# One pass over all tokens, layouts prepared on the host, and sums of squares on VectorE, in a two-layer decoder step on eight cores

## The chip, the cores and the metric

The kernel runs on all eight cores of one Trainium2 chip. Each core works on one prompt of 2048 tokens and on 128 sample tokens, and nothing is exchanged between cores. The metric is the device time of the slowest core in microseconds (us). Engines are named as in the profile: PE is TensorE (matmul), PEld its weight loads, DVE VectorE, ACT ScalarE, POOL GpSimd, SP SyncE.

Executions of a program on eight cores fall into two states. In the slow one the cores of one die, or of both, show a lower granted clock and the time is some per cent longer. Only fast runs are compared here.

## The reference

Activations are `x` with 1024 features. Weights are shared by prompt and sample tokens.

```python
def _swiglu(h, w_gate, w_up, w_down):            # 1024 -> 2816 -> 1024
    return (jax.nn.silu(h @ w_gate) * (h @ w_up)) @ w_down

for layer in range(2):
    x = x + 0.5 * _swiglu(_rmsnorm(x, norm_g[layer, 0]), ...)
    h = _rmsnorm(x, norm_g[layer, 1])
    # even layer: gelu(h @ w_u) * spatial_gate(layernorm(gelu(h @ w_v)))
    #             beside a gated 3-tap causal convolution; then @ e_w_out
    # odd layer:  p = h @ o_w_in; causal means of the last 2, 4, 8, 16 rows
    #             minus p; per group @ pool_w, * pool_scale; then @ o_w_out
    x = x + mixer(h)
    x = x + 0.5 * _swiglu(_rmsnorm(x, norm_g[layer, 2]), ...)
y = _rmsnorm(x, final_norm_g)
```

There are four feed-forward stages (FFN), one even and one odd mixer, and seven norms.

## The kernel before

The tokens are cut in two halves of 1024 and 1152, and the whole network runs first on one, then on the other, so every weight is read twice. Activations live transposed (features on partitions). Three parts matter for the argument.

`x` arrives row by row and is transposed by TensorE, 136 times; `y` goes back the same way.

```python
def tr(e, i=i, half=half, bk=bk):
    for k in range(4):
        c = half * 4 + k
        ins = e.transpose(banks[bk][:, k * 128:(k + 1) * 128],
                          big[:, i * 1024 + c * 128:i * 1024 + (c + 1) * 128], ident[:])
    return ins
```

A norm needs, for each token, the sum of squares over 1024 features. ScalarE squares each of the eight chunks of 128 features, and TensorE adds them up, across chunks and across partitions, by multiplying with a matrix of 1/1024. Six of the seven norms do this; the last one's squares are summed by ScalarE, after the transposes of `y`:

```python
P.add("act", ... e.activation(out=buf, in_=xT[:, dc, a:a + n], func=AF.Square), ...)
P.add("pe",  ... e.matmul(bank[:, 0:n], onesm[:], buf, start=(dc == 0), stop=(dc == NCH - 1)), ...)
```

The down projection of an FFN runs all 22 chunks of hidden features into one bank (PSUM, where matmuls accumulate), and VectorE adds the result to `x` once:

```python
for f in range(f0, f1):
    ins = e.matmul(po[:, 0:n], sd[:, f, :], aT[:, f, a:a + n], start=(f == 0), stop=(f == NF - 1))
...
P.add("dve", ... e.scalar_tensor_tensor(out=xT[:, dc, a:a + n], in0=po[:, 0:n], scalar=0.5, in1=xT[:, dc, a:a + n], ...))
```

## Time and profile before

| | before |
|---|---|
| time, median of the first 5 runs | 2565.91 us (2562.0 to 3019.57) |
| profiled span, slowest core | 2561.0 us |
| TensorE busy, matmuls | 2430.3 us, 13009 |
| TensorE idle | 131 us |
| VectorE busy | 792.0 us |
| read from memory | 337.63 MB |

The run of 3020 us is slow. The lines behind the table stand in the prediction below. To read them: a busy TensorE is not a TensorE at its peak, so the time is split in three parts. First come columns times their spacing (the stream), then busy time above that spacing (mostly matmuls at about double the spacing, called half clock here), then idle time.

### The profile page before, as it was taken

To read this page: it belongs to the slowest core of one execution; us is meant where nothing else is said; L and a number is where in the kernel's file an instruction comes from. 1 tells how busy PE (TensorE), PEld (TensorE's weight loads), DVE (VectorE), ACT (ScalarE), POOL (GpSimd) and SP (SyncE) were. 2 spreads that over 40 slices of the span, in tenths; PEclk is the share of its full clock that TensorE was granted. 3 is DMA by queue.
4 is the path that set the end of the run, shared out by engine and by line. 5 is a ranking of instruction groups with operands and counts; after the bars stand their busy time and mean duration, and the time that the engine had idled before them with its cause. 6 is when DMAs were issued, how large, how long until landed. Compare 5 with 4: busy or idle time off the path is not lost.

```text
span 2561.0 us, 35190 instructions; the slowest of 8 cores (2545.0 to 2561.0 us)
## 1 busy us (share of the span) xinstructions
PE 2430.3 (95%) x13009; PEld 1287.6 (50%) x13009; DVE 792.0 (31%) x1329; ACT 597.3 (23%) x1134; POOL 305.7 (12%) x319
## 2 busy tenths in 40 slices
PE   6999899999999889997899989999999999899997
PEld 3444344444444334444466645566655665456664
DVE  3211553112221552113322147522132212742213
ACT  3111322112111242102311132411121111531102
POOL 2101111111101111111010102111111111001110
PEclk8999999999999999998899999999999999999998
DMA  8667366567566555668255544555675555436472
GB/s 149 83 67 73 42 91 82 68 65 91 67 72 68 74 66 67 72 72 174 58 72 58 59 58 63 90 67 62 58 87 67 61 55 67 59 50 82 57 75 77
DMA packets 418126, 187.20 MB, mean 73 GB/s; under 512 B 186251, under 2 KB 412119, under 8 KB 417944
## 3 DMA queue, kind: packets, MB, share of 16 engines
q0 software_dynamic: 410048, 162.55, 54.3%
q1 hardware_dynamic: 6616, 17.69, 2.1%
q10 hardware_dynamic: 1296, 4.72, 0.6%
q8 instruction: 108, 1.77, 0.3%
q14 instruction: 58, 0.48, 0.1%
HBM read 337.63 MB, written 10.29 MB: 136 GB/s over the span
## 4 chain that ended last, share of the span: by engine, by line
PE 87%; DVE 5%; ACT 2%; issue 2%; DMA 2%; SPq 1%; POOL 1%; ACTq 0%; DVEq 0%; POOLq 0%
PE ps L529 25%; PE ps L532 25%; PE ps L573 24%; PE ps L637 4%; DVE hT L504 2%; PE ps L482 2%; PE ps L928 1%; DVE big L949 1%; PE ps L808 1%; PE ps L704 1%; PE ps L750 1%; PE ps L810 1%; DMA big<-xs 1%; PE ps L831 1%; SPq L392 1%
## 5 line engine op out<-in xcount | busy, mean ns | idle before, releaser
L529 PE MATMUL ps<-hT,wslot 128*128 128x384 bf16 (+1 forms) x3520 | 723.6, 349 | 15.7 <-DVE big L538 15.0
L532 PE MATMUL ps<-hT,wslot 128*128 128x384 bf16 (+1 forms) x3520 | 721.9, 348 | 0.0
L573 PE MATMUL ps<-big,wslot 128*128 128x384 bf16 (+1 forms) x3520 | 659.5, 348 | 0.0
L538 DVE TENSOR_TENSOR big<-ps,stmp 128x384 bf16<-128x384 f32 (+1 forms) x440 | 268.2, 611 | 1015.9 <-ACT stmp L536 1008.5
L529 PEld LDWEIGHTS ps<-hT,wslot 128*128 128x128 bf16 x3520 | 344.6, 98 | 322.7 <-issue 23.7
L532 PEld LDWEIGHTS ps<-hT,wslot 128*128 128x128 bf16 x3520 | 345.5, 98 | 305.9 <-issue 5.5
L573 PEld LDWEIGHTS ps<-big,wslot 128*128 128x128 bf16 x3520 | 345.7, 98 | 304.2 <-issue 3.4
L536 ACT ACTIVATE stmp<-ps 128x384 f32<-128x384 f32 (+1 forms) x440 | 234.6, 533 | 1024.8 <-PE ps L532 1023.1
L578 DVE SCALAR_TENSOR_TENSOR xT<-ps,xT 128x384 f32<-128x384 f32 (+1 forms) x160 | 97.6, 610 | 495.3 <-PE ps L573 479.9
L473 ACT ACTIVATE sqbuf<-xT 128x384 bf16<-128x384 f32 (+1 forms) x240 | 131.8, 563 | 499.9 <-DVE xT L578 416.8
L299 POOL DMA_DIRECT2D wslot<-wg x88 | 77.2, 878 | 1162.0 <-PE ps L532 804.6
L299 POOL DMA_DIRECT2D wslot<-wd x64 | 85.9, 1342 | 711.3 <-PE ps L532 413.0
L504 DVE SCALAR_TENSOR_TENSOR hT<-xT,cT,rs 128x384 bf16<-128x384 f32 (+1 forms) x240 | 145.5, 668 | 65.1 <-ACT rs L495 64.0
L482 PE MATMUL ps<-sqbuf,onesm 128*128 128x384 bf16 (+1 forms) x240 | 76.5, 373 | 15.9 <-ACT sqbuf L473 15.2
L299 POOL DMA_DIRECT2D wslot<-wu x88 | 78.0, 887 | 0.0
L928 PE MATMUL ps<-hT,wslot 128*128 128x384 bf16 (+1 forms) x320 | 62.6, 359 | 5.3 <-DVE big L892 5.3
L637 PE MATMUL ps<-mixT,wslot 128*128 128x384 bf16 (+1 forms) x320 | 65.0, 347 | 2.4 <-DVE xT L641 2.4
L641 DVE TENSOR_TENSOR xT<-ps,xT 128x384 f32<-128x384 f32 (+1 forms) x80 | 48.5, 608 | 60.5 <-PE ps L637 60.5
L637 PE MATMUL ps<-hT,wslot 128*128 128x384 bf16 (+1 forms) x320 | 65.6, 350 | 0.2 <-ACT hT L1005 0.2
L949 DVE TENSOR_TENSOR big<-big 128x1038 f32<-128x1038 f32 (+3 forms) x40 | 49.4, 1236 | 10.2 <-ACT big L933 7.7
L1045 ACT ACTIVATE rt<-ps 128x512 f32<-128x512 f32 x17 | 10.0, 587 | 171.1 <-PE ps L1040 161.0
L928 PEld LDWEIGHTS ps<-hT,wslot 128*128 128x128 bf16 x320 | 32.1, 101 | 35.3 <-issue 10.0
(134 smaller groups left out, 968.6 us busy)
## 6 DMA issues: line engine op xcount, KB each, us to landing
wslot<-wg POOLq DMA_DIRECT2D x88, 512.0 KB, 6.2
wslot<-wu POOLq DMA_DIRECT2D x88, 512.0 KB, 8.1
wslot<-wd POOLq DMA_DIRECT2D x64, 704.0 KB, 7.9
wslot<-ewin POOLq DMA_DIRECT2D x16, 512.0 KB, 7.4
big<-xp SPq DMA_DIRECT2D x8, 512.0 KB, 10.1
wslot<-ewout POOLq DMA_DIRECT2D x8, 512.0 KB, 8.8
wslot<-owin POOLq DMA_DIRECT2D x8, 512.0 KB, 7.1
wslot<-owout POOLq DMA_DIRECT2D x8, 512.0 KB, 6.8
```

The lines of the kernel that those rows point to most:

```text
L299: res.append(e.dma_start(out=dst, in_=src))
L473: P.add("act", lambda e, dc=dc, a=a, n=n, buf=buf: e.activation(out=buf, in_=xT[:, dc, a:a + n], func=AF.Square), r=K("x", dc, a, n), w=[( ...
L482: P.add("pe", lambda e, dc=dc, n=n, buf=buf, bank=bank: e.matmul(bank[:, 0:n], onesm[:], buf, start=(dc == 0), stop=(dc == NCH - 1)), r=[( ...
L504: P.add("dve", lambda e: e.scalar_tensor_tensor(out=dst, in0=xT[:, c, a:a + n], scalar=cT[:, nidx * 8 + c:nidx * 8 + c + 1], in1=rs[:, 0:n ...
L529: e.matmul(pg[:, 0:n], sg[:, c, fi * 128:(fi + 1) * 128], hT[:, c, a:a + n], start=(c == 0), stop=(c == NCH - 1))
L532: ins = e.matmul(pu[:, 0:n], su[:, c, fi * 128:(fi + 1) * 128], hT[:, c, a:a + n], start=(c == 0), stop=(c == NCH - 1))
L536: P.add("act", lambda e, k=k, n=n, pg=pg: e.activation(out=stmp[k][:, 0:n], in_=pg[:, 0:n], func=AF.Silu), r=[("ps", k)], w=[("stmp", k)])
L538: P.add("dve", lambda e, k=k, f=f, a=a, n=n, pu=pu: e.tensor_tensor(out=aT[:, f, a:a + n], in0=pu[:, 0:n], in1=stmp[k][:, 0:n], op=ALU.mul ...
L573: ins = e.matmul(po[:, 0:n], sd[:, f, :], aT[:, f, a:a + n], start=(f == 0), stop=(f == NF - 1))
L578: P.add("dve", lambda e, dc=dc, a=a, n=n, po=po: e.scalar_tensor_tensor(out=xT[:, dc, a:a + n], in0=po[:, 0:n], scalar=0.5, in1=xT[:, dc, ...
L637: ins = e.matmul(po[:, 0:n], sw[:, c, (di % 2) * 128:(di % 2 + 1) * 128], src[:, c, a:a + n], start=(c == 0), stop=(c == NCH - 1))
L928: ins = e.matmul(pb[:, 0:n], sw[:, c, (di % 2) * 128:(di % 2 + 1) * 128], hT[:, c, a:a + n], start=(c == 0), stop=(c == NCH - 1))
```

## The change

Its intent is to shorten TensorE's stream and to keep it fed. The new kernel makes one pass over all 2176 tokens in five blocks, so weights are read once. The host delivers `x` already transposed and takes `y` transposed, and it packs the weights in the order in which they are used. The sums of squares move to VectorE, and only the last step, across partitions, stays on TensorE, in the type float32r (fp32r below). The tile for hidden features holds 8 of the 22 chunks for 2176 tokens, so FFN and down projection run in three parts, each with its own addition to `x`. The product of the pool weights and the output weights of the odd mixer is formed first. The causal sums become a scan. The diff, cut to its core:

```diff
-SBS = [dict(idx=0, Tp=1024, Ts=0, T=1024, poff=0, blocks=[(0, 512), (512, 512)]),
-       dict(idx=1, Tp=1024, Ts=128, T=1152, poff=1024, blocks=[(0, 384), (384, 384), (768, 384)])]
+BL = [(0, 384), (384, 512), (896, 384), (1280, 512), (1792, 384)]
+PARTS = [(0, 6), (6, 8), (14, 8)]            # hidden chunks per part
...
-    # x: DMA by rows, 136 transposes on PE, copies out by ACT and DVE
+    P.add("sp", ... e.dma_start(out=xT(o0, o1), in_=x_in[:, o0:o1]) ...)      # host has transposed it
...
-    P.add("pe", ... e.matmul(bank[:, 0:n], onesm[:], buf, start=(dc == 0), stop=(dc == NCH - 1)) ...)  # 8 per block
+    P.add("dve", ... e.tensor_tensor(out=acc(0, n), in0=acc(0, n), in1=dst, op=ALU.add) ...)           # 7 per block
+    P.add("pe", ... e.matmul(banks[bk][:, 0:n], ones_t[:], accr_t[k][:, 0:n], start=True, stop=True) ...)  # 1 per block, fp32r
...
-    # odd mixer: doubling additions for the causal sums, pool weights on all tokens, scale, output weights
+    P.add("dve", ... e.tensor_tensor_scan(out=S_(0, pn), data0=pext(16 + a, ...), data1=pext(16 + a - w_, ...),
+                                          op0=ALU.add, op1=ALU.subtract) ...)
+    # V = (pool_w * pool_scale) @ o_w_out, 32 matmuls of 512 columns, then one projection with V
```

Normalizations (`x * g * rs`, one VectorE instruction per chunk) wait in a queue `hq`. The last down part takes one out per group, but only while block 0 has some. The rest follows when the next stage asks for them.

```python
last_rate[0] = 2 if final else (1 if any(x[0] == 0 for x in hq) else 0)
down(j0 if dc < 4 else j1, b, dc, nf, True)      # ends with tick(last_rate[0]): so many out of hq
```

## The prediction

> **What bounds the kernel now.** First the page, then the granted clocks, then the windows, then the chain that ended last, then the waits of TensorE.
>
> ```profile
> span 2561.0 us, 35190 instructions; the slowest of 8 cores (2545.0 to 2561.0 us)
> ...
> PE 2430.3 (95%) x13009; PEld 1287.6 (50%) x13009; DVE 792.0 (31%) x1329; ACT 597.3 (23%) x1134; POOL 305.7 (12%) x319
> ...
> HBM read 337.63 MB, written 10.29 MB: 136 GB/s over the span
> ...
> PE 87%; DVE 5%; ACT 2%; issue 2%; DMA 2%; SPq 1%; POOL 1%; ACTq 0%; DVEq 0%; POOLq 0%
> ```
>
> TensorE is busy for 95% of the span and no other engine passes 31%; the chain that ended last is TensorE work for 87%. The kernel is bound by its matmul stream, so a change can win in only two ways: fewer matmul columns, or less time in which TensorE is idle or at a low clock. The chain in order of time gives the rate of the stream:
>
> ```profile
> 60.37 1.73 PE ps L529 x8
> ...
> 214.48 9.50 PE ps L573 x44
> ...
> 1410.05 1.30 PE ps L532 x8
> ...
> 1438.49 10.72 PE ps L573 x66
> ```
>
> Columns: start, length, what. A 512-column matmul takes 1.73 / 8 = 216 ns, a 384-column one 10.72 / 66 = 162.4 ns. The larger means in the list of groups (348 ns) are latencies of overlapping instructions and are not used. With the block widths 512, 512 | 384, 384, 384 of before the mean is (2 x 216.2 + 3 x 162.4) / 5 = 183.9 ns. The windows show where the time is that is not this stream:
>
> ```profile
> core 1: us, PE busy (x) PEld busy (x) DVE busy (x) ACT busy (x) POOL busy (x), PEclk, DMA share, GB/s
> 0.00:60.00 60.00, 39.98 (x169) 21.94 (x170) 21.27 (x33) 21.82 (x37) 13.43 (x26) 0.89 0.93 159
> 60.00:195.00 135.00, 135.00 (x627) 61.23 (x626) 26.98 (x39) 23.29 (x39) 16.28 (x17) 1.00 0.59 71
> ...
> 260.00:370.00 110.00, 98.11 (x457) 43.98 (x455) 66.54 (x114) 37.02 (x57) 22.30 (x22) 0.95 0.48 64
> ...
> 875.00:960.00 85.00, 76.88 (x327) 31.84 (x326) 53.23 (x70) 35.19 (x62) 8.74 (x10) 0.92 0.48 62
> ...
> 1190.00:1242.00 52.00, 30.97 (x148) 18.96 (x146) 23.45 (x42) 25.12 (x63) 1.75 (x2) 0.71 0.67 189
> ```
>
> Inside a feed-forward stage (60 to 195) TensorE is busy for 135 of 135 us at clock 1.00: nothing to win there except columns. The idle time, 2561 - 2430 = 131 us, lies at the start, in the mixers (260 to 370, 875 to 960 and their second copies), at the seam between the two halves of the tokens (1190 to 1242: 21 us idle, clock 0.71) and at the end. Few of the waits are for data from memory:
>
> ```profile
> PE ps L482 <- ACT sqbuf L473: 15.2, 9, 3.1
> PE ps L529 <- DVE big L538: 15.0, 8, 2.5
> PE ps L432 <- DMA big<-xp: 12.1, 6, 3.3
> ```
>
> The first is the norm statistics, the second the product that frees a bank, the third the load of x, not of weights.
>
> **What the Trainium skill says.** (1) "TensorE: Matmul & The Clock Gate", section "Wait — 56ns, not 53.3ns?": warm matmuls follow each other after N / 2.4 GHz + about 2.5 ns, 215.7 ns for 512 columns. The trace agrees (216). So after, as before, width alone sets the stream. (2) Same page, "HAM oscillation — how this bites in real kernels": after gaps of more than about 3.4 us the array restarts at half clock. The trace agrees in kind: clock 0.71 to 0.95 just in the windows with gaps. (3) "FP8 and Floating Point Precision", "TensorE Precision Notes": true fp32 takes four passes, reduced precision reads fp32 and truncates. So I count the new float32r statistics as one pass; no run here shows it yet. (4) "DVE: opcode table, instruction layouts, handler registers and perf-mode slots", "Datapath and trigger behaviour": the built-in scan runs at half throughput, two cycles an element. The trace before has no scan.
>
> **The change, part by part.** It is a rewrite around one pass over all 2176 tokens (blocks 384, 512, 384, 512, 384: same mean width, 183.9 ns) where before there were two passes over 1024 and 1152.
>
> 1. Unchanged stream. Feed-forward: 4 x 528 x 5 = 10560 matmuls x 183.9 = 1942 us on both sides. Projections of the mixers: before 640 + 320 + 640 = 1600 at 183.9 = 294 us, the v tiles 136 x 216 = 29, the spatial gate about 7. All stay.
>
> 2. Removed from TensorE: 136 + 136 fp32 transposes of x and y, which the host layout replaces (23.8 + 21.0 us busy) and the small ones (about 6); 240 statistics matmuls (44 us) become 7 norms x 5 blocks = 35 (6.4 us), because VectorE now adds up the squares; the 80 pool-weight matmuls (14.7 us) become 2 x 8 x 2 = 32 of 512 columns that multiply the two weight matrices (6.9 us). Before: 1942 + 294 + 29 + 7 + 51 + 44 + 15 = 2382 us. After: 1942 + 294 + 29 + 7 + 6 + 7 = 2285 us. That is 97 us less, all of it on the chain. Check: busy 2430 - 2382 = 48 us is half-clock time, so the kernel before loses 131 + 48 = 179 us beyond its stream.
>
> 3. Weights are read once, not twice, in rows of 8 to 16 KB made by the host. Reads fall from 338 to about 138 (feed-forward) + 23 (mixers) + 9 (x) + 3 = 173 MB. TensorE waited for no weights, so this is hidden and worth about nothing, except at the start.
>
> 4. The seam at 1190 and half of the mixer entries and exits vanish. What replaces the 179 us, stage by stage:
>    - Start: x block 0 (1.57 MB) beside the first weights, at the 269 GB/s that the trace shows from 13 to 24 us, about 15 us; then squares, sum, statistics, Ln, Exp and eight normalizations of 0.61 us: about 10. First gate matmul near 25 us (before: 41). Block 1 has to land before ScalarE, in order, gets on: 1.57 + 2.1 + 4.2 MB of x and weights at 269 GB/s is 29 us, near 33 us in all, and its norm ends near 45, while block 0's work ends near 35. Another 12 us or so. Together 37.
>    - Even mixer: per v tile VectorE does 0.69 + 0.18 + 2 x 0.75 + 0.69 = 3.06 us, 17 tiles are 52 us, plus the 32 normalizations that the last stage left over, x 0.67 = 21: 73 us against 29 + 29 + 4 = 62 us of TensorE. The convolution after it needs 2.6 us of VectorE per 4.4 us of TensorE and absorbs part. Loss 8.
>    - Odd mixer: the doubling adds (1.24 us each for 1024) become a scan of 435 elements: estimate from the skill, 870 / 0.96 + 156 ns = 1.06 us. 30 x (1.06 + 0.61) + 10 x 0.61 + samples about 9 + 21 for left-over normalizations = 86 us, against 59 + 7 us of TensorE. Loss about 22.
>    - End: the last down projection has per block and output 0.61 (residual) + 0.60 (sum of squares) + 0.67 (final norm) = 1.88 us of VectorE against 8 x 183.9 = 1.47 us of TensorE. 72 against 59 us, then the last statistics (about 4) and the last store (about 4): 21.
>    - Seams between the other stages 10, half clock after the gaps 15 (before 48).
>    Sum 37 + 8 + 22 + 21 + 25 = 113.
>
> 5. Added work on VectorE. Down projection in three parts: residual additions 160 -> 480 at 0.61 us = +195 us; sums of squares 245 x 0.60 = +147; more normalizations (280, not 240) +24; copies out of transposes and final scaling about -38; pool about equal. 792 + 328 = about 1120 us, 47% of the span. In the feed-forward stages it fits: a gate-up pair has 2.94 us of TensorE for one product (0.61) and at most two normalizations (1.34); a middle down group has 1.10 to 1.47 us for one addition; the last one 1.47 us for 1.21. Eight rotating banks carry the jitter. So it costs only where step 4 says so.
>
> Sum: 2285 + 113 = 2398 us of span, about 2400 as measured (the timed median was 5 us above this profiled span, the profiled run itself 2 us).
>
> **The rivals.** (a) VectorE becomes the bound more widely. In order, and with little margin in the last down part (1.21 of 1.47) and in the first feed-forward, which also normalizes (12.0 of 11.8 us per block). If each of five norm seams loses 10 us more: 2450. For it: VectorE grows by 40%; against: 31% now, and the overloaded stretches are short. (b) The start is bound by memory: all of x, 8.9 MB, and 4.2 MB of weights have to land in the first feed-forward stage, 13.1 MB / 159 GB/s (the mean of the first 60 us before) = 82 us instead of 49 at 269: +25, so 2425. Against: the rows are longer now. (c) A denser stream makes the clock limiter act: one of five timed runs before took 3020 us. The ratio there is 3020 / 2562 = 1.18; a run wholly in that state would be near 2285 x 1.18 + 113 = 2810. Against: dense windows before show 1.00, and only fast runs are compared. (d) The losses of step 4 overlap with the stream better than I count, and the mixers lose nothing: 2285 + 37 + 21 + 15 = 2360.
>
> **Range and chances.** (d) sets the lower side, (a) and (b) the upper. I predict 2400 us, 2350 to 2455 in 8 of 10 cases. To miss a 2% gain (2515 us) the new losses would have to reach 230 us, more than before's 179. Faster by over 2%: 0.95; within 2%: 0.035; slower: 0.015, left for an effect like the limiter or a four-pass float32r with long waits.
>
> **What would show it.** Right: a matmul count near 12400 with no transposes and 35 statistics matmuls of about 184 ns spacing; 162 and 216 ns spacings unchanged; TensorE busy near 2300 us at 96% or so; VectorE near 1120 us; reads near 173 MB; first gate matmul near 25 us; the largest idle before the odd mixer's input matmuls, released by VectorE; a scan of 512 elements near 1.2 us. Wrong: large idle of gate or down matmuls behind VectorE (rival a), behind x from memory beyond 50 us (b), a granted clock below 0.95 throughout (c), or weights that come late with a window of idle at each seam, which step 3 excludes.

## The result, and the profile after

The kernel after takes 2405.88 us in the median of nine runs (2403.08 to 2708.24; the slowest is slow), beside 2565.3 us for before on the same chip. The ratio of the fast runs is 0.9379, with a 95% interval of 0.937 to 0.9388. A ratio here is the mean time of one kernel's fast runs over that of the other's of the same rounds, so it is not quite the ratio of the quoted medians. The time fell inside the predicted range, 6 us from its centre.

The page of the kernel after:

```profile
span 2403.4 us, 33263 instructions; the slowest of 8 cores (2400.2 to 2403.4 us)
...
PE 2303.4 (96%) x12431; PEld 1217.5 (51%) x12431; DVE 1068.1 (44%) x1813; ACT 534.2 (22%) x970; POOL 92.8 (4%) x140
...
HBM read 174.89 MB, written 11.08 MB: 77 GB/s over the span
...
PE 89%; DVE 5%; issue 2%; ACT 1%; DMA 1%; POOL 1%; DVEq 0%; SPq 0%; ACTq 0%; POOLq 0%
```

TensorE lost 127 us of busy time, VectorE gained 276 us, and the kernel is still bound by TensorE. The chain that ended last (start, length, what) shows the stream between the mixers:

```profile
2.89 18.48 DMA xT<-x
...
98.79 397.26 PE ps L410 x2168
...
782.53 431.69 PE ps L410 x2344
```

2344 matmuls in 431.69 us without a break are 184.2 ns each, which is the mean of the spacings read off before (183.9 ns). So each matmul costs what it did; there are fewer of them.

The windows of the kernel after, cut at its stages. Columns as in the prediction: the stretch, its length, then busy time (instructions) of PE, PEld, DVE, ACT and POOL, then PEclk, DMA share and GB/s. They are the start, the rest of the first pass over the blocks, the even mixer, the odd mixer and the end:

```profile
0.00:30.12 30.12, 0.66 (x2) 0.32 (x2) 8.55 (x19) 6.15 (x12) 2.69 (x9) 1.00 0.94 215
30.12:98.79 68.67, 56.76 (x261) 26.74 (x262) 45.94 (x81) 40.29 (x65) 2.88 (x4) 0.95 0.45 117
...
541.90:618.75 76.85, 61.54 (x342) 31.14 (x341) 69.10 (x110) 23.13 (x43) 43.16 (x48) 0.93 0.02 4
...
1737.50:1812.60 75.10, 56.26 (x279) 28.03 (x277) 69.38 (x114) 23.79 (x53) 0.53 (x1) 0.89 0.30 71
...
2337.00:2403.40 66.40, 41.88 (x221) 21.53 (x218) 52.79 (x94) 22.09 (x39) 0.00 (x0) 0.88 0.33 135
```

In the other five windows TensorE is busy from end to end: its whole idle time, 100 us, is in these five. In the two mixers VectorE is busy for 69 of 77 and 69 of 75 us, so there it is VectorE that sets the pace. The waits of TensorE (waiter, released by: total us, times, longest) name the work:

```profile
PE ps L458 <- DVE accr L449: 41.3, 8, 23.5
PE ps L410 <- DVE hT L481: 26.1, 8, 7.9
...
PE ps L641 <- DVE scr L620: 7.6, 4, 3.8
```

The first are norm statistics at the start and at the end of the kernel. The second are normalizations: 8.6 us (4 times) in the first FFN and 17.5 us (4 times) at the odd mixer's entry. The third is the gate's layer norm in the even mixer.

### The profile page after: what moved, and what is told of

Read it like the earlier page. It is cut to its first block, busy times and chain, and to the rows that moved or that the text cites. A ratio compares the mean times of both kernels' runs of the same rounds, so it can differ in the third digit from the quotient of the medians.

```text
span 2403.4 us, 33263 instructions; the slowest of 8 cores (2400.2 to 2403.4 us)
## 1 busy us (share of the span) xinstructions
PE 2303.4 (96%) x12431; PEld 1217.5 (51%) x12431; DVE 1068.1 (44%) x1813; ACT 534.2 (22%) x970; POOL 92.8 (4%) x140
## 4 chain that ended last, share of the span: by engine, by line
PE 89%; DVE 5%; issue 2%; ACT 1%; DMA 1%; POOL 1%; DVEq 0%; SPq 0%; ACTq 0%; POOLq 0%
PE ps L410 89%; DVE hT L481 2%; DMA xT<-x 1%; DVE xT L481 1%; DVE scr L840 1%; ACT nrm L433 0%; DVE xT L539 0%; DVE nrm L440 0%; PE ps L458 0%; DVE scr L620 0%; DVE scr L647 0%; POOL misc L609 0%; POOL mid L651 0%; DVE accr L449 0%; ACT nrm L466 0%
## 5 line engine op out<-in xcount | busy, mean ns | idle before, releaser
L410 PE MATMUL ps<-hT,ws 128*128 128x384 bf16 (+1 forms) x8000 | 1488.6, 349 | 32.0 <-DVE hT L481 26.1
L410 PEld LDWEIGHTS ps<-hT,ws 128*128 128x128 bf16 x8000 | 784.9, 98 | 730.3 <-issue 51.4
L410 PE MATMUL ps<-mid,ws 128*128 128x384 bf16 (+1 forms) x4160 | 771.2, 347 | 0.0
L526 DVE TENSOR_TENSOR mid<-ps,scr 128x384 bf16<-128x384 f32 (+1 forms) x440 | 268.7, 611 | 939.7 <-PE ps L410 930.5
L410 PEld LDWEIGHTS ps<-mid,ws 128*128 128x128 bf16 x4160 | 405.1, 98 | 358.0 <-issue 4.4
L521 ACT ACTIVATE scr<-ps 128x384 f32<-128x384 f32 (+1 forms) x440 | 233.8, 533 | 1401.9 <-PE ps L410 1389.4
L539 DVE SCALAR_TENSOR_TENSOR xT<-ps,xT 128x384 f32<-128x384 f32 (+1 forms) x480 | 291.6, 610 | 258.3 <-PE ps L410 258.1
L433 ACT ACTIVATE nrm<-xT 128x384 f32<-128x384 f32 (+1 forms) x280 | 155.9, 565 | 240.8 <-DVE xT L539 144.7
L481 DVE SCALAR_TENSOR_TENSOR hT<-xT,misc,nrm 128x384 bf16<-128x384 f32 (+1 forms) x240 | 147.9, 664 | 15.6 <-ACT nrm L468 15.6
L440 DVE TENSOR_TENSOR nrm<-nrm 128x384 f32<-128x384 f32 (+1 forms) x210 | 126.5, 602 | 22.1 <-ACT nrm L433 18.4
L458 PE MATMUL ps<-accr,onesr 128*128 128x384 f32 (+1 forms) x35 | 18.4, 525 | 41.4 <-DVE accr L449 41.3
```

The lines of the kernel that those rows point to most:

```text
L410: ins = e.matmul(banks[bk][:, 0:n], l, rr, start=(i == 0), stop=(i == len(pairs) - 1))
L433: P.add("act", lambda e, dst=dst, b=b, c=c: e.activation(out=dst, in_=xs(b, c), func=AF.Square), r=[xk(b, c)], w=[dk])
L440: P.add("dve", lambda e: e.tensor_tensor(out=acc(0, n), in0=acc(0, n), in1=dst, op=ALU.add), r=[dk, acc.key(0, n)], w=[acc.key(0, n)])
L458: P.add("pe", lambda e: e.matmul(banks[bk][:, 0:n], ones_t[:], accr_t[k][:, 0:n], start=True, stop=True), r=[("accr", k), ("ones",)], w=[( ...
L481: P.add("dve", lambda e: e.scalar_tensor_tensor(out=dst, in0=xs(b, c), scalar=g, in1=q(0, n), op0=ALU.mult, op1=ALU.mult), r=[xk(b, c), q. ...
L521: P.add("act", lambda e: e.activation(out=s_(0, n), in_=banks[kg][:, 0:n], func=AF.Silu), r=[("ps", kg)], w=[s_.key(0, n)])
```

## The experiments

Ten kernels ran, and all gave correct results. Each starts from the kernel after; edits are shown against it. In the first batches the kernel before took 2565 to 2568 us. For the kernel after the fast runs lie between 2403.1 and 2406.8 us, with a median of 2405.7. It was not run again beside the experiments, which ran on four chips, and the median of before differs by 3 us between undisturbed batches. A difference of 2 or 3 us from 2405.7 is therefore not resolved.

### 1. Every weight read twice again

Is halving the weight traffic worth anything? The first four items aside, each weight is loaded twice into the same place.

```diff
             P.add("pool", lambda e, o_=o_, i_=i_: [e.dma_start(out=o_, in_=i_)], ...)
+            if j >= NSLOT:
+                P.add("pool", lambda e, o_=o_, i_=i_: [e.dma_start(out=o_, in_=i_)], ...)
```

> Every weight item after the first four is read from memory twice, one load behind the other into the same buffer, so that reads return to about 320 MB, near the 338 MB of the kernel before. My theory (the halved weight traffic is hidden and worth nothing): an item takes 2 x 8.8 = 18 us to land, its predecessor is used for about 29 us, so the time stays within 5 us of 2406. Rival (part of the gain is relief of memory and of the DMA engines, whose share fell from 0.5 to 0.2): 20 to 60 us slower, with matmul spacings above 162.4 and 216 ns or waits of matmuls for weights.

Measured: 2415.89 us in the median, ratio 0.9438 [0.9369, 0.9506]. The interval is wide because one of the four runs took 2449.54 us, with a clock of 0.967 to 0.982 on one die. The page and the chain of this run:

```profile
HBM read 328.51 MB, written 11.08 MB: 141 GB/s over the span
```

```profile
99.11 397.26 PE ps L412 x2168
...
530.83 8.46 DMA ws<-wall
540.35 12.41 DMA ws<-wall
...
789.64 431.69 PE ps L412 x2344
```

With 154 MB more, the two long stretches take 397.26 and 431.69 us, to the hundredth what they took after. So the traffic itself cost the stream nothing. The time is 10 us more all the same, between the two stated ranges. By the starts of the long stretches 7 us of it lie before the end of the even mixer's stage (782.53 us in the kernel after, 789.64 here) and 4 in the odd mixer's. At the even mixer's entry the chain waits for a doubled load on GpSimd's queue, which also has to compute there. That order is made by the test: the second load waits for the first on the queue that does the gate's arithmetic. What the 4 us are was not traced.

### 2. More work for VectorE in the FFN

Is VectorE's extra work free inside the FFN, as the prediction has it? The middle of the three down parts gets one useless addition per group, 160 in all.

```diff
+            if pad:
+                P.add("dve", lambda e: e.tensor_tensor(out=acc(0, n), in0=acc(0, n), in1=sq[0](0, n), op=ALU.add), ...)
-                            down(j, b, dc, nf, False)
+                            down(j, b, dc, nf, False, pi == 1)
```

> In the middle down projection of each feed-forward stage one more VectorE addition of 0.60 us per group, 160 in all, 96 us of VectorE work. My theory (VectorE has room in the feed-forward stages, so the residual additions that the split in three added cost nothing): 1.21 us of VectorE per 1.47 us of TensorE, time within 4 us of 2406, VectorE busy 1068 + 96 = 1164 us. Rival (VectorE work is paid for everywhere, through banks that come free later): 30 to 96 us slower.

Measured: 2406.62 us (2405.42 to 2407.93), ratio 0.9369 [0.9354, 0.9384]. The page:

```profile
PE 2304.1 (96%) x12431; PEld 1217.9 (51%) x12431; DVE 1151.6 (48%) x1973; ACT 534.1 (22%) x970; POOL 92.6 (4%) x140
```

VectorE is busy for 83.5 us more and the time is within the scatter of the kernel after. VectorE does not bound the middle down part, even with this load added.

### 3. The transposes put back

272 fp32 transposes of 128 x 128 go into the gate and up stage of the second FFN, four to a bank, with no reader.

```diff
+                        if (l, w) == (0, 1) and pc["tr"] < 68:
+                            ...
+                            def tr(e, bt=bt, b=b):
+                                for k in range(4):
+                                    o = xoff(b, 2 * k)
+                                    ins = e.transpose(banks[bt][:, k * 128:(k + 1) * 128], xT(o, o + 128), ident[:])
+                                return ins
```

> 272 fp32 transposes of 128 x 128, as many as the host layout removed, put back among the gate and up matmuls of the second feed-forward stage, results unread. My theory (columns taken off TensorE's stream come back one for one): slower by their 23.8 + 21.0 = 45 us as the busy time of the kernel before gave it, or less if that busy time counts latencies, not below 272 x 56 ns = 15 us. Rival (the transposes stood beside other work and cost nothing): within 5 us of 2406.

Three of the five timed runs were slow (2543.94, 2597.54 and 2768.06 us); the fast ones took 2434.43 and 2437.02 us, and the profiled span is 2432.9 us. Against the 2403.4 us of after that is 29.5 us. In the trace the transposes start 109 ns apart, and 272 x 109 ns is 29.7 us. So they lie on the path one for one, as predicted, at less than the 45 us of the prediction. In this run the line of the group is no guide to the cost:

```profile
L583 PE MATMUL ps<-ident,xT 128*128 128x128 f32 x272 | 40.8, 273 | 0.0
```

The mean of 273 ns in this line (columns: busy us, mean ns, idle before) is a latency of overlapping instructions, and the busy time takes in the tail of each group of four, under which the next matmul already runs. In the kernel before the 45 us were right, for another reason. Two lines of its timeline:

```profile
2522.34 1.91 PE L1040 MATMUL ps<-ident,xT 128*128 128x128 f32 x16
2527.52 1.94 PE L1040 MATMUL ps<-ident,xT 128*128 128x128 f32 x8 [3.27 <-ACT misc L1048]
```

Sixteen transposes take 1.91 us at one place, and after a wait eight take 1.94 at another. Those that follow each other start 110 ns apart in the median, but 98 of the 271 recorded for `x` and `y` are followed at about 210. That is a low clock: at the start of before the distance falls from 213 to 109 ns at 17.6 us, where the granted clock rises to 1.00 in the trace, with nothing but transposes on TensorE up to there. From each one's start to the next start, idle time left out, they take 23.8 + 20.1 = 44 us. Some 30 us of these are columns, 11 the low clock in the stages where before had them, and 3 the ends of transposes after which TensorE sat idle. This test puts back the columns only.

### 4. All sums of squares back on TensorE

```diff
+            if self.nidx in PEN:                       # here PEN = all seven norms
+                q = sqb[pc["sb"] % 4]
+                P.add("act", ... e.activation(out=q(0, n), in_=xs(b, c), func=AF.Square) ...)
+                def mm(q=q, i=i, b=b):
+                    P.add("pe", ... e.matmul(banks[bk][:, 0:n], onesb[:], q(0, n), start=(i == 0), stop=(i == NCH - 1)) ...)
+                at(2, mm)
+                return
```

> The sums of squares of all seven norms go back to TensorE as in the kernel before (280 bf16 matmuls with ones, in two reserved banks), VectorE's 245 additions and the 35 float32r matmuls go. My theory: TensorE's stream grows by 245 x 183.9 ns = 45 us; the last stage, where VectorE was the bound (72 us of VectorE against 59 of TensorE), gives back about 13 and the first stage a few: 25 to 35 us slower, VectorE busy near 920 us. Rival (the additions on VectorE cost as much as they saved): 0 to 10 us slower or faster.

Measured: two fast runs took 2492.81 and 2493.11 us, 87 us more than after and far above both ranges that were expected. A third took 2525.93 with one die's clock down to 0.97. The ratio is 0.9748 [0.9671, 0.9825], and against before the verdict at 2% is unclear. The waits of TensorE, and VectorE at the end of an FFN (start, length, what):

```profile
PE ps L444 <- ACT nrm L438: 69.4, 39, 9.8
```

```profile
1290.48 0.56 DVE L567 SCALAR_TENSOR_TENSOR xT<-ps,xT 128x384 f32<-128x384 f32 x1 [0.82 <-PE ps L416]
1290.95 5.38 DVE L509 SCALAR_TENSOR_TENSOR hT<-xT,misc,nrm 128x512 bf16<-128x512 f32 x8
1296.25 1.02 DVE L567 SCALAR_TENSOR_TENSOR xT<-ps,xT 128x384 f32<-128x384 f32 x2
```

245 matmuls of 183.9 ns are 45 us. TensorE is busy for 2371.0 us, 68 more than after, and idle for 120 us, 20 more; the rest of the busy time is matmuls at more than their spacing. When eight normalizations come out of the queue in one burst, the addition to `x` behind them is late by 5.38 us, ScalarE cannot square, and TensorE, which works in order, stands at the statistics matmul though it has other work behind it. With the sums on VectorE, TensorE is not idle at these FFN ends at all in the kernel after. But this is not a clean measure of the change. Before had other queues and other bursts, and only six norms on TensorE; the edit also reserves two of the eight banks for the sums, and what that costs was not tested. Experiments 7 and 8 together give a cleaner one.

### 5. The start: block 0 of x ahead of the weights

The first gate matmul of after begins at 30.12 us, 5 us later than predicted, and block 0 of `x` lands at 21.4. The first weights share the DMA engines with it. Here most of them wait until that block has landed.

```diff
+            if (j, k_) == (0, 1):
+                after = late
...
-    load_item(0)
-    load_item(1)
+    x0k = [xT.key(0, NCH * n0)]
+    load_item(0, late=x0k)
+    load_item(1, after=x0k)
```

> Order of the first loads only: the second half of the first weight item and the second item are issued when block 0 of x has landed, so that they do not share the DMA engines with it. My theory (the start is bound by memory: block 0 of x landed at 21.4 us because 4.2 MB of weights ran beside it, and the gate matmuls began at 30 us): block 0 lands near 13 us, the first gate matmul comes near 21 us, and 5 to 9 us are gained. Rival (what comes after binds anyway, since the same 7.9 MB must land before block 1 can be normalized): the first gate matmul comes earlier but the gap before block 1 grows by as much, 0 to 2 us.

Measured: 2407.24 us, ratio 0.9381 [0.9364, 0.9398]: no gain. The timeline of TensorE (start, length, what, and in brackets the idle time before and its releaser):

```profile
23.22 4.96 PE L412 MATMUL ps<-hT,ws 128*128 128x384 bf16 x16 [5.95 <-DVE misc L922]
...
37.76 4.52 PE L412 MATMUL ps<-hT,ws 128*128 128x384 bf16 x16 [5.00 <-DMA ws<-wall]
47.05 11.89 PE L412 MATMUL ps<-hT,ws 128*128 128x384 bf16 x47 [4.78 <-DMA ws<-wall]
```

The first gate matmul comes 7 us earlier, and then TensorE waits for weights, 5.00 and 4.78 us. The stage ends at 101.4 us against 98.8. So the order of the loads does not bind the start. That the sum of their bytes does fits these waits, but no run changed the bytes.

### 6. GpSimd out of the gate of the even mixer

In the trace of after one VectorE instruction of the layer norm takes 1123 ns in the mean, and it is long where GpSimd works beside it. The first fence shows VectorE with GpSimd busy, then idle; the second the GpSimd instruction beside the first:

```profile
569.42 1.16 DVE L616 SCALAR_TENSOR_TENSOR mid<-mid,misc,scr 128x512 f32<-128x512 f32 x1
...
577.02 0.74 DVE L616 SCALAR_TENSOR_TENSOR mid<-mid,misc,scr 128x512 f32<-128x512 f32 x1
```

```profile
568.76 1.27 POOL L651 TENSOR_TENSOR mid<-scr,mid 128x512 bf16<-128x512 f32 x1 [1.38 <-DVE scr L647]
```

To test that, the gate's bias is added on TensorE by one fp32r matmul, and VectorE multiplies straight out of the bank. The GpSimd product is gone for the 16 prompt tiles.

```diff
+                if not sidx:
+                    e.matmul(banks[bk][:], ones_t[:], bsr_t[:], start=True, stop=False)
...
+            if not sidx:
+                P.add("dve", lambda e: e.tensor_tensor(out=o3, in0=banks[bk][:].rearrange(...), in1=u3, op=ALU.mult), ...)
+                return
```

> In the even mixer the bias of the gate is added by a float32r matmul with a matrix of ones, and VectorE multiplies by u straight from PSUM (as many VectorE operations as before), so the 16 multiplications on GpSimd go. My theory (VectorE's operations with two SBUF inputs wait while GpSimd multiplies: line 616's took 1123 ns in the mean, but 740 when GpSimd was idle): the mean falls to about 750, VectorE's work in the stage falls by 7.8 us and the time by 5 to 8 us, less 4 us more of TensorE. Rival (the longer operations are their own, for instance the reading of the mean as a scalar): 1123 stays and the time grows by 0 to 4 us.

Measured: 2399.43 us (2399.17 to 2399.76), ratio 0.9352 [0.9335, 0.9369], some 6 us faster than after. The same instruction, before and after the edit (busy us, mean ns):

```profile
L616 DVE SCALAR_TENSOR_TENSOR mid<-mid,misc,scr 128x512 f32<-128x512 f32 x17 | 19.1, 1123 | 0.0
```

```profile
L617 DVE SCALAR_TENSOR_TENSOR mid<-mid,misc,scr 128x512 f32<-128x512 f32 x17 | 12.4, 731 | 0.2 <-issue 0.2
```

The instruction itself is unchanged and takes 731 ns: the 390 ns more were GpSimd's company. TensorE's idle time in the even mixer's stage fell from 15.3 to 6.1 us. The Trainium skill, "GPSIMD Engine Reference", section "1. Specifications", says that GpSimd's interfaces to on-chip memory are shared with VectorE, with contention for VectorE instructions that have two inputs there. This one has two, and the trace agrees.

### 7. Three norms on TensorE, and normalizing earlier

The sums for the norms ahead of both mixers and for the last one go to TensorE. In addition the blocks of the first two are normalized as soon as they are ready (one normalization per group while any is in the queue), rather than at the mixer's entry.

```diff
+    PEN = (1, 4, 6)          # with the code of experiment 4
+    RATE = (1, 4)
-    last_rate[0] = 2 if final else (1 if any(x[0] == 0 for x in hq) else 0)
+    last_rate[0] = 2 if final else (1 if (hq if nxt in RATE else any(x[0] == 0 for x in hq)) else 0)
```

> Sums of squares on TensorE only for the norms before the two mixers and the final one, and for the first two of these VectorE normalizes blocks 0 to 3 already within the last down projection. From the run with all seven on TensorE, a norm costs about 40 x 0.225 - 5 x 0.37 = 7 us of stream, so +21 for three. My theory (VectorE is the bound in both mixers and in the last stage): the idle time there, 15.3 + 18.8 + 24.5 = 59 us, falls by 35 to 45, net 10 to 30 us faster than 2406. Rival (the in-order wait of TensorE for each square costs more than it frees, as in the run with all seven, which lost 85 us): 10 to 40 us slower.

Measured: the fast runs are at 2409.46 and 2409.94 us, ratio 0.9392 [0.9372, 0.9412]; the other two were slow. Both stated ranges missed (10 to 30 us faster, 10 to 40 slower). TensorE:

```profile
PE 2329.1 (97%) x12536; PEld 1223.6 (51%) x12536; DVE 1017.8 (42%) x1709; ACT 537.1 (22%) x970; POOL 91.8 (4%) x140
```

Idle time fell from 100 to 79 us and busy time rose by 26: the gain at the mixers and the cost of 105 more matmuls cancel. The run mixed two edits, so the next one takes the second alone.

### 8. Normalizing earlier, sums on VectorE

```diff
-    last_rate[0] = 2 if final else (1 if any(x[0] == 0 for x in hq) else 0)
+    last_rate[0] = 2 if final else (1 if (hq if nxt in (1, 4) else any(x[0] == 0 for x in hq)) else 0)
```

> Only the timing of the normalizations is changed: in the last down projection ahead of each of the two mixers every finished block is normalized at once, one per group, instead of block 0 alone; the sums of squares stay on VectorE. If the mixers' idle time is left-over normalizations (24 to 32 at 0.67 us, some 16 to 21 us of VectorE at each entry), the gaps at both entries shrink without the columns that the run with TensorE sums added: 2396 to 2402 us against 2406, the odd gap from 19 to about 8. If VectorE has no room in the last down projection (0.61 + 0.60 + 0.67 = 1.88 us of work per 1.47 us group), the wait only moves from the mixer to the down projection: 2404 to 2412 us, the odd gap shrinks but TensorE waits for VectorE inside the projection before it.

Measured: the fast runs took 2394.54, 2395.78 and 2396.66 us (the other three were slow), ratio 0.9307 [0.9243, 0.9372]. That is 10 us under after, from one line, and at the lower edge of what the first theory expected. TensorE's idle time fell from 15.3 to 9.8 us in the even mixer and from 18.8 to 13.5 in the odd one, where 8 was expected. The waits for normalizations:

```profile
PE ps L410 <- DVE hT L481: 18.4, 6, 6.2
```

They were 26.1 us, 8 times, in the kernel after. The part at the odd mixer's entry is 9.8 us here and was 17.5. In the odd mixer's window (from the last matmuls of the FFN ahead of it) VectorE had 32 normalizations to do in the kernel after, and 17 here:

```profile
L481 DVE SCALAR_TENSOR_TENSOR hT<-xT,misc,nrm 128x512 bf16<-128x512 f32 x16 | 10.8, 744 | 0.0
L481 DVE SCALAR_TENSOR_TENSOR hT<-xT,misc,nrm 128x384 bf16<-128x384 f32 x16 | 8.6, 610 | 0.0
```

```profile
L481 DVE SCALAR_TENSOR_TENSOR hT<-xT,misc,nrm 128x512 bf16<-128x512 f32 x8 | 5.6, 746 | 0.0
L481 DVE SCALAR_TENSOR_TENSOR hT<-xT,misc,nrm 128x384 bf16<-128x384 f32 x9 | 4.9, 614 | 0.0
```

The rival, that VectorE has no room in the last down part (durations of 1.88 us in a group of 1.47) and the wait only moves, is refuted as to the time: TensorE is busy for 54.00 of 54 us from 1683 to 1737. VectorE at the end of that part in this run:

```profile
1734.85 0.55 DVE L539 SCALAR_TENSOR_TENSOR xT<-ps,xT 128x384 f32<-128x384 f32 x1
1735.32 0.55 DVE L440 TENSOR_TENSOR nrm<-nrm 128x384 f32<-128x384 f32 x1
1735.79 0.61 DVE L481 SCALAR_TENSOR_TENSOR hT<-xT,misc,nrm 128x384 bf16<-128x384 f32 x1
1736.32 0.55 DVE L539 SCALAR_TENSOR_TENSOR xT<-ps,xT 128x384 f32<-128x384 f32 x1
...
1741.07 0.55 DVE L539 SCALAR_TENSOR_TENSOR xT<-ps,xT 128x384 f32<-128x384 f32 x1
```

The three take 0.55 + 0.55 + 0.61 = 1.71 us by their lengths, but the next round begins 1.47 us after the first: each starts about 80 ns before the one ahead of it has ended in the record. The Trainium skill, "Perfetto Trace Analysis", section "Optimizing Scalar/DVE Operations", says that the fixed access cost of an instruction shows in its profiled latency about twice over, since the half in which the write is acknowledged overlaps with the next instruction. The trace agrees in kind, with 80 ns of overlap. So the lengths, added up, are not the engine's time. In one point the rival was right. A round of 1.47 us is longer than TensorE's 8 x 162.4 ns = 1.30 us at this width, and VectorE is busy for 11.77 of the 12 us up to 1737. TensorE's last down matmul ends at 1736.8, and VectorE's last addition starts at 1741.07. That VectorE is full here fits the 13.5 us that remain, but no run separates it.

Against experiment 7 (2409.46), which has the same timing of normalizations and three norms' sums on TensorE, this run is 14 us faster by the middle of its fast runs. The two are not of the same rounds or chip, and in the rounds of this run the fast runs of before scatter from 2565 to 2585 us. The intervals of the ratios (0.9392 and 0.9307) touch at 0.9372, so the size is known to a few us only. The two reserved banks of experiment 7 are in the difference too. With that reserve it is the cleanest measure of the moved sums: three norms are worth about 14 us. In proportion the six that before had on TensorE would be some 28, which is an estimate.

### 9. The gate bias and one norm on TensorE

The edits of experiment 6 together with those of experiment 7 for the norm ahead of the odd mixer alone (PEN = RATE = (4,)).

> The gate bias on TensorE (which alone gave 2399.4 us) together with TensorE sums for the norm ahead of the odd mixer alone, whose blocks are then normalized early. The norm on TensorE costs 35 more column matmuls, 6.4 us of columns and some waiting; the odd gap, 19 us, should fall to about 8 as in the run with three such norms. Theory that both gains add and the columns cost only their width: 2393 to 2397 us. Rival that the sums on TensorE give everything back through waits in its order, as the run with three norms hints: 2398 to 2404 us.

Measured: the fast runs took 2395.05 to 2395.72 us, ratio 0.9308 [0.9259, 0.9357], in the middle of the first theory's range. The bias alone gave 2399.4, so the norm added 4 us of gain. Whether the sums or the timing gave it, this run does not say.

### 10. The gate bias and normalizing earlier

The edits of experiments 6 and 8, with all sums on VectorE.

> The two edits that each gained alone, the gate bias on TensorE (2399.4 us, some 6.5 under the changed kernel's 2406) and the earlier normalization ahead of both mixers (2395.3 us, some 11 under), with all sums of squares on VectorE. If the two act on different waits, the gains add: 2387 to 2391 us. They overlap in the even mixer, where both relieve VectorE: if the bias only moves the same wait there, 2392 to 2396 us. The run of the bias together with one norm's sums on TensorE gave 2395.2, so a result under 2392 also says that the sums are better left on VectorE.

Measured: 2385.5 us in the median (fast runs 2384.91 to 2387.33, one slow run), ratio 0.929 [0.9278, 0.9303]. This beats both kernels, after by 20 us and before by 7.1%. The waits for the even mixer's layer norm were 7.6 us in the kernel after and are now

```profile
PE ps L642 <- DVE scr L621: 1.3, 1, 1.3
```

The two edits gained 6 and 10 us alone and gain 20 together, at least their sum, so they do not act on the same wait. The range of the theory that the gains add was 2387 to 2391. The excess is small beside the spread between chips, but a further effect is possible: the granted clock in the even mixer's window is 0.93 in the kernel after, 0.95 with either edit alone, and 1.00 here. This run is also 10 us better than experiment 9, in which the sums for one norm are on TensorE and only one mixer is normalized early. That comparison changes two things. It fits experiments 7 and 8, by which the sums are better left on VectorE, and does not prove it.

## Why the prediction was right

**The bound and the stream.** Right. The spacing of a matmul is unchanged (184.2 ns in the mean), the count is 12431 (predicted near 12400), and TensorE is busy for 2303.4 us (2300).

**Transposes.** Right. The term in step 2 of the prediction, 23.8 + 21.0 us, was taken from busy times, though the prediction itself warns against lengths for matmuls. It came out right: in the trace of before these transposes take 44 us from start to start (experiment 3). But step 2 books all of it as columns, and only some 30 us are. The other 14 are low clock and ends before gaps, in the stages that had the transposes.

**Statistics.** The columns of three norms are 105 x 183.9 ns = 19 us by the same count. Experiments 7 and 8 measure about 14 for three, so the sums moved gave back somewhat less than their columns. That the 35 fp32r matmuls space at 184 ns was wrong: in the trace of after the matmul behind one starts 0.37 us later in the median. 35 times the difference is 6.5 us, too little to matter for the total. Its distance hardly grows with the width (368 ns for 384 columns, 372 for 512), so it is not more passes over the columns.

**Weights once, worth about nothing.** Right, shown by experiment 1.

**VectorE's added work is hidden in the FFN.** Right, shown by experiment 2 for the middle down part. The predicted 1120 us were 1068.1: I had added up lengths of instructions that overlap by some 80 ns, as experiment 8 shows. The lengths of all VectorE instructions in the trace of after add up to 1124.9 us.

**The losses, stage by stage.** The windows give 118 us against 113. The idle time is the length of a window less PE's; the half clock is 2303.4 less the predicted stream of 2285:

| | predicted | measured |
|---|---|---|
| start | 37 | 29.5 + 11.9 = 41.4 |
| even mixer | 8 | 15.3 |
| odd mixer | 22 | 18.8 |
| end | 21 | 24.5 |
| other seams | 10 | 0.0 |
| half clock | 15 | 18 |

The start was mis-sized in one term: block 0 of `x` landed at 21.4 us, not 15, for the first weights share the DMA engines with it. Experiment 5 shows that reordering moves the wait and does not remove it, so a small part of rival (b) was real. The even mixer lost twice what was predicted, since 0.75 us was taken for an instruction that takes 1.12 beside GpSimd; experiment 6 shows it.

The odd mixer's mechanism, left-over normalizations, was named in the prediction. Experiment 8 bears it out in part: with 17 of the 32 left, the idle time fell from 18.8 to 13.5 us. A scan of 512 elements took 1282 ns in the trace (predicted near 1.2 us), one of 256 took 747, so an element costs 2.1 ns. A two-input instruction beside it took 0.69 us for 512 and 0.56 for 384, 1.0 ns an element; half throughput, as the prediction quoted it, is confirmed.

Two sums of the prediction do not come out: the odd mixer's 86 against 59 + 7 us is 20 and not 22, and rival (b)'s 82 instead of 49 us is 33 and not 25. Neither matters for the centre. The other seams cost nothing: the errors of +12 and -10 nearly cancel, and part of the closeness of 2400 to 2406 is such luck. The half-clock term is a remainder, and about 6 us of it are the fp32r matmuls above. The sign that the largest idle time would stand before the odd mixer's input matmuls came only in part: within the mixers it does (18.8 us), but the start and the end idle for longer.

**The rivals.** (a) A VectorE bound more widely: refuted by experiment 2 for the middle down part, and for the last one by TensorE's idle time of 0 there. VectorE binds in the mixers and at the end only, but with the normalizations of experiment 8 it is full in the last part too. (c) The limiter: the kernel after held a granted clock of 0.989 in its fast run, before 0.974 to 0.978; slow runs occur with both kernels. (d) Mixers that lose nothing: wrong by 34 us.

**Where the 157.6 us between the two profiled spans went.** Taking in both traces each matmul's distance to the next start, with idle time left out, gives this account:

| | before | after | difference |
|---|---|---|---|
| transposes (44 for `x` and `y`, 9 small ones) | 53 | 0 | 53 |
| statistics matmuls | 44 | 13 | 31 |
| pool weights | 15 | 7 | 8 |
| bf16 matmuls beyond their spacing (low clock, ends before gaps) | 50 | 15 | 35 |
| idle time | 131 | 100 | 31 |

The rows add up to 158. The first three are the prediction's 97 us of stream (92 here), the last two its 179 - 113 = 66 us of losses (66 here). By the windows, idle time fell from 21 to 0 at the seam and from 61 to 34 in the mixers. It rose from 20 to 41 at the start and from 15 to 25 at the end. The other 14 us, spread over before's stages, are gone.

**What stays open.** This says where the time was, not what each part of the rewrite is worth. Experiments bear out some 30 us for the transposes and about 14 for three norms. No experiment put a second pass back, so that the single pass removed the 66 us of losses is argued and not shown. Nor is it known how much of the 87 us of experiment 4 the kernel before would have had.

## What to carry to other kernels

When an engine's stream is the bound, price a removed instruction at the distance between starts, not at its length in the profile, and take that distance in the stage where it stands: the same transposes were 110 ns apart in one place and 210 in another. Where the bound engine works in order, it also pays to free it from waiting for its neighbours' small results: in experiment 8 that alone gave 10 us, with no column taken away. After a large change look again at short stretches in which another engine has become the bound; here one line that spreads work into a stage with some room, and one product taken off GpSimd, were worth 20 us more.

## What the Trainium skill lacked or had wrong

- "GPSIMD Engine Reference", section "1. Specifications", states the contention of VectorE with GpSimd without a number of its own. Here a VectorE instruction with two 128x512 fp32 inputs on chip took 1123 ns in the mean beside GpSimd and 731 without. Where a GpSimd product was running, the VectorE instruction ended about 0.55 us after it (five cases between 560 and 588 us in the timeline of the kernel after).
- "TensorE: Matmul & The Clock Gate", Part 4, gives 275 to 390 ns for a 128x128 bf16 transpose. Its latency is not its cost: fp32 transposes took 273 ns each by their records here, but started 109 ns apart, and 272 of them cost 29 us. In the kernel before many started 210 ns apart.
- The same page, Part 1, advises to budget 13/16 of the clock for dense matmuls on all cores, on the default power profile (this chip's profile is not on record). The fast runs of the kernel after held 0.987 or more on all eight cores with TensorE busy for 96%. Clocks below 0.96 (down to 0.80 in the mean of a core) came in the slow state alone, mostly on one die.
- "FP8 and Floating Point Precision" led me to count an fp32r matmul as one bf16 pass. The matmul behind one started 0.37 us later in the median, against 0.18 for bf16. The page gives no number of passes for the reduced read. The distance is 368 ns for 384 columns and 372 for 512, which speaks against further passes; whether it is a wait or the longer weight load (199 ns in the record) was not separated.
